# Indexer keys of the sample group: four page gathers and a DRAM round trip in place of 48 gathers and 32 register-addressed transfers

## The chip, the cores and the metric

The kernel runs on one core of one Trainium2 chip. The metric is the device time of one execution in microseconds, as the median of three runs. The kernel before takes 2734.93 us (2734.37 to 2735.12).

## What is computed

The reference is one inference step of a two-layer decoder trunk: layer 0 is sparse attention with an indexer, layer 1 a convolution module, each followed by a gated feed-forward block with a short convolution. A prompt of 256 tokens and a sample group of 8 sequences with 4 tokens each go through the same weights, 288 columns in all. Only the indexer of the sample group touches the change: each sequence has 2048 past positions in 16 pages of 128, and the pages lie anywhere in a pool of 160.

```python
ki_past = cache_ki[page_table].reshape(Bd, PAST_LEN, IDX_DIM)       # 8 x 2048 x 64
dots  = jnp.einsum('thd,sd->ths', qi, ki, ...)                      # 16 index heads
score = jnp.einsum('th,ths->ts', wi * IDX_W_SCALE, jax.nn.relu(dots))
_, idx = lax.top_k(jnp.where(causal, score, -jnp.inf), k_sel)       # 256 of 2052
```

The keys and values at `idx` are then gathered and attended to. Everything else is matrix products with weights that are read once.

## The kernel before

**Products with weights.** `K.pump` (L135) loads a weight slab of 128 x 1024 numbers (512 KB) with one DMA on SP's queue (L145) into one of five `raw` buffers, then splits it into a high part `wh` (ACT, L159) and a low part `wl` (DVE, L161), three buffers of each. `K.gemm_gen` (L187) runs three matmuls of 288 columns for each 128 x 128 block: `wh` with `xh` (L228), `wh` with `xl` (L229), `wl` with `xh` (L230). A slab of the first stage has two rows of four blocks, 24 matmuls. While PE works on slab i, loads are issued up to slab i + 4 and splits up to slab i + 2; a split for slab i + 3 needs the buffers that PE frees when it has finished slab i.

**Order of the other work.** All instructions are issued in the order of the program text. Side work is written as Python generators in lanes (`Lane`, L103). Each step of a product calls `tick` (L167), which adds the step's estimated time to every lane's credit (at most 3.0); a lane with positive credit runs its generator to the next `yield`, and the yielded number is taken off the credit. In one tick the lanes come in the order `ev`, `norms`, `bg`, `bg2`. So a `yield 6.0` means: go on after about 6 us worth of matmuls, by the program's own estimate. An engine then executes its instructions strictly in this order, and a wait in one holds what is behind it on that engine.

**The first stage** runs `g_idx[0]` (L732, slabs 0 and 1, 80 columns: index key and head weights), `g_idx[1]` and `g_idx[2]` (L1028, eight slabs each, index queries: slabs 2 to 9 and 10 to 17), then `g_k`, `g_q`. The lane `ev` turns the new index keys (`ropes`, L688) and then stores them: `post_ki` (L735) issues `out_kidx` on POOL's queue (L738). The lane `bg` holds `load_kx` (L670) and behind it `sample_index` (L802), whose 16 index products read the past index keys `kx` (L833).

**The past index keys.** `kiT` holds each page transposed, 64 rows of 128 numbers (512 bytes a row). Four tiles `kx[pr]` of 128 x 2048 hold two sequences each, 64 partitions per sequence, positions along the row. Twelve of the 16 pages of each sequence come by 48 gathers on POOL's queue (L665 to L668, through `gather`, L659): one gather fetches 128 rows of 512 bytes by a table of row numbers `idxI` (L647 to L652) and fills one 128 x 128 block. The last four pages of each sequence come by 32 transfers on SP's queue (L670 to L679): SP loads the page number from `tab` into a register (`value_load`, L676) and issues a DMA of 64 x 512 bytes from that address (L677). Two of these come with each step of the generator, between the weight loads on the same queue.

Of the kernel before, what the change touches and what calls it, by code (L numbers as in the profile page):

```python
# [7 lines left out]
F32 = mybir.dt.float32  # L8
F32R = mybir.dt.float32r
BF = mybir.dt.bfloat16  # L10
I32 = mybir.dt.int32
I16 = mybir.dt.int16
AF = mybir.ActivationFunctionType
OP = mybir.AluOpType
# [5 lines left out]
NS, TS = 8, 4  # L20
T = TP + NS * TS
NH, HD, NKV, GQ = 16, 128, 4, 4
NI, ID = 16, 64
PAST, PAGE = 2048, 128
NPG = PAST // PAGE
POOL = 160
# [14 lines left out]
CAP = 3.0  # L41
SDEL = 6
TOPK = 2.6
KG = 12
DGP = 6.0
NDG = 14
CQ = 287
BIS = (1.6, 0.2)
DOTS = 0.35
ROPE = 0.8  # L50
# [483 lines left out]
def trunk(ctx, tc, a, o, stages=9):  # L534
    k = K(ctx, tc, a, o)
    nc = k.nc
# [61 lines left out]
    ap = st.enter_context(tc.tile_pool(name="attn", bufs=1))  # L598
# [9 lines left out]
    bp = stB.enter_context(tc.tile_pool(name="idx", bufs=1))  # L608
# [7 lines left out]
    def split_tiles(j, n):  # L616
        for i in range(j, j + n):
            k.split_x(xh[:, i, :T], xl[:, i, :T], xs[:, i])
# [7 lines left out]
    load_x(12, 4)  # L626
    tab = bp.tile([128, 128], I32, name="tab")
    pt = a["page_table"]
    io = bp.tile([128, 3], F32, name="io")
    nc.gpsimd.dma_start(tab, bass.AP(tensor=pt.tensor, offset=pt.offset, ap=[[0, 128], [1, 128]]))  # L630
    nc.gpsimd.dma_start(io, a["iota"])
    coni = bp.tile([128, 2 * T], F32, name="coni")
    con = bp.tile([128, NCO], F32, name="con")

# [8 lines left out]
    split_tiles(0, 1)  # L643
    k.pump(-2)
    split_tiles(1, 3)

    tabI = bp.tile([128, 4, NPG], I32, name="tabI")  # L647
    idxI = bp.tile([128, 64], I32, name="idxI")
    tab3 = tab.rearrange("p (b g) -> p b g", g=NPG)
    for s in range(2):  # L650
        nc.vector.tensor_copy(tabI[s * 64:(s + 1) * 64], tab3[s * 64:(s + 1) * 64, s::2, :])
    nc.vector.tensor_scalar(idxI, tabI.rearrange("p a b -> p (a b)"), float(ID), io[:, 2:3], op0=OP.mult, op1=OP.add)  # L652
    split_tiles(4, 4)
    k.pump(-1)
    nc.sync.dma_start(coni, a["consts_i"])
# [3 lines left out]
    def gather(out, src, idx):  # L659
        nc.gpsimd.indirect_dma_start(out=out, out_offset=None, in_=src,  # L660
                                     in_offset=bass.IndirectOffsetOnAxis(ap=idx, axis=0))


    kx = [kvA.tile([128, 2, 1024], F32, name="kvt").rearrange("p a b -> p (a b)") for _ in range(4)]
    for g0 in range(0, KG, 2):  # L665
        for pr in range(4):
            for g in range(g0, g0 + 2):
                gather(kx[pr][:, g * 128:(g + 1) * 128], a["kiT"], idxI[:, pr * NPG + g:pr * NPG + g + 1])  # L668

    def load_kx():  # L670
        kp = a["kiT"].rearrange("(a d) c -> a d c", d=ID)
        for pr in range(4):
            for g in range(KG, NPG):
                for s_ in range(2):
                    c = (2 * pr + s_) * NPG + g
                    r = nc.sync.value_load(tab[0:1, c:c + 1], min_val=0, max_val=POOL - 1)  # L676
                    nc.sync.dma_start(kx[pr][64 * s_:64 * s_ + 64, g * 128:(g + 1) * 128],  # L677
                                      kp[bass.ds(r, 1)].rearrange("a d c -> d (a c)"))
                yield 2.9  # L679

    k.bg.append(load_kx())

# [119 lines left out]
    def sample_index():  # L802
# [63 lines left out]
        nc.vector.tensor_scalar(scr, S, 0.0, 0.0, op0=OP.is_ge, op1=OP.add, accum_out=cnt)  # L866
        yield BIS[0]
        p = total()
        yield BIS[1]
        nc.vector.tensor_scalar(v, p[:, :1], float(KSEL_S), -1.0, op0=OP.is_lt, op1=OP.mult)  # L870
        for bit in range(30, -1, -1):
# [4 lines left out]
            nc.vector.tensor_scalar(scr, S, cand.bitcast(F32), 0.0, op0=OP.is_ge, op1=OP.add, accum_out=cnt)  # L876
            yield BIS[0]
            p = total()
            yield BIS[1]
            fl = sp.tile([128, 1], I32, name="fl", bufs=2)  # L880
# [8 lines left out]
        nc.vector.tensor_scalar(eq, S, thr, 0.0, op0=OP.is_equal, op1=OP.add, accum_out=ce)  # L889
        yield BIS[0]  # L890
        p = total()
# [179 lines left out]
    for gi in range(2):  # L1071
# [6 lines left out]
        for tt in range(3):  # L1078
            n = 128 if tt < 2 else 32
            p = bank("tr", 3)  # L1080
# [182 lines left out]
    for t in range(n_t + 1):  # L1263
        if t == n_t - 8:
            k.pump(g_out[0].first)
        if t < n_t:
            if t % TS == 0:
                b = t // TS
# [256 lines left out]

    spread = tc.dram_tile([last * 128, CQ], F32, name="spread")
    zero = fp.tile([128, last, CW], F32, name="zero")
# [178 lines left out]
def _consts():  # L1706
    f = np.float32
    c = np.zeros((128, NCO), f)

    def put(n, v, p0=0):  # L1710
        o_, w_ = CO[n]
        c[p0:p0 + v.shape[0], o_:o_ + w_] = v

    p = np.arange(128)
    same = (p[:, None] % 32) == (p[None, :] % 32)
    put("bones", same.astype(f))
    put("lower", (same & (p[:, None] // 32 < p[None, :] // 32)).astype(f))
    hrow = (p % 64) // TS
    put("esel", (np.arange(NI)[:, None] == hrow[None, :]).astype(f), 64)
    tok = (2 * np.arange(4)[None, :, None] + (p // 64)[:, None, None]) * TS + (p % TS)[:, None, None]  # L1720
    put("wmask", ((tok == np.arange(32)[None, None, :]) * IDX_W).astype(f).reshape(128, 128))
    pos = np.concatenate([np.arange(TP), np.tile(PAST + np.arange(TS), NS)]).astype(f)

    def angles(rot):
        inv = np.power(f(500000.0), (-np.arange(0, rot, 2, dtype=f) / f(rot)).astype(f)).astype(f)
        ang = (pos[:, None] * inv[None, :]).astype(f)
        return np.cos(ang).T.astype(f), np.sin(ang).T.astype(f)

    cs, sn = angles(32)
    put("cq", np.tile(np.concatenate([cs, cs]), (4, 1)))  # L1730
    put("sq", np.tile(np.concatenate([-sn, sn]), (4, 1)))
    cs, sn = angles(16)
    ci = np.concatenate([np.tile(np.concatenate([cs, cs, np.ones((48, T), f)]), (2, 1)),
                         np.tile(np.concatenate([-sn, sn, np.zeros((48, T), f)]), (2, 1))], axis=1)
    put("tri", (p[None, :] > p[:, None]).astype(f))
    put("ncaus", np.where(np.arange(TS)[None, :] <= (np.arange(32) % TS)[:, None], 0.0, NEG).astype(f), 96)
    r = np.arange(32)
    put("blk", (r[:, None] // TS != r[None, :] // TS).astype(f), 96)
    put("oneb", ((p % 32)[:, None] // TS == np.arange(NS)[None]).astype(f))
    put("seg", np.tile(-float(PAGE) * np.arange(4, dtype=f), (128, 1)))  # L1740
    put("pow", np.tile(2.0 ** np.arange(8), (128, 1)).astype(f))
    put("tapm", (p[:, None] % 32 == np.arange(32)[None]).astype(f))
    put("tokr", np.where(r[:, None] == np.arange(144)[None] // GQ, NEG, 0.0).astype(f), 96)
    iota = np.stack([p, p % 32, p % 64], 1).astype(f)
    return c, np.ascontiguousarray(ci), iota, np.arange(512, dtype=f)


def _layout(inp):
    g = {n: np.asarray(v) for n, v in inp.items()}
    c = np.ascontiguousarray  # L1750
    a = {}
    a["xT"] = c(np.concatenate([g["x_prompt"].reshape(TP, D), g["x_sample"].reshape(NS * TS, D)]).T)
    a["kvc"] = np.concatenate([g["cache_k"][0].reshape(POOL * PAGE, NKV * HD),
                               g["cache_v"][0].reshape(POOL * PAGE, NKV * HD)], axis=1)
    a["kiT"] = c(g["cache_kidx"][0].transpose(0, 2, 1)).reshape(POOL * ID, PAGE)
    sc = np.zeros((D, NS, CW - 1 + TS), np.float32)
    sc[:, :, :CW - 1] = g["state_conv"][0].transpose(2, 0, 1)
    a["scT"] = c(sc.reshape(NT, 128, -1).transpose(1, 0, 2)).reshape(128, -1)
    a["stT"] = c(g["state_ffn"].transpose(0, 3, 1, 2)).reshape(2, FF, NS * 2)
    a["page_table"] = c(g["page_table"]).reshape(-1)  # L1760
    for n in ("w_attn_in", "w_attn_out", "w_pw1", "w_pw2"):
        a[n] = c(g[n][0])
    for n in ("w_ffn_gate", "w_ffn_up", "w_ffn_down"):
        a[n] = c(g[n])
    cols = {}
    fm = lambda v: v.reshape(-1, 128).T
    for n in ("b_pw1", "b_dw", "ln_conv_g", "ln_conv_b", "b_pw2"):
        cols[n] = fm(g[n][0])
    for n in ("ln_mix_g", "ln_mix_b", "ln_ffn_g", "ln_ffn_b"):
        for l in range(2):  # L1770
            cols[f"{n}{l}"] = fm(g[n][l])
    cols["w_dw"] = g["w_dw"][0].reshape(CW, NT, 128).transpose(2, 1, 0).reshape(128, NT * CW)

    wq = np.concatenate([np.zeros((1, D), np.float32), g["w_dw"][0]]).reshape(8, 4, NT, 4, 32)
    a["w_dq"] = c(wq.transpose(1, 4, 2, 3, 0).reshape(128, NT * 32))
    for l in range(2):
        cols[f"w_c{l}"] = g["w_ffn_conv"][l].reshape(3, NF, 128).transpose(2, 1, 0).reshape(128, NF * 3)
        cols[f"b_c{l}"] = fm(g["b_ffn_conv"][l])
    a["pvec"] = c(np.concatenate([cols[n] for n in PV], axis=1))
    a["consts"], a["consts_i"], a["iota"], a["iota512"] = _consts()  # L1780
    a["ident"] = np.eye(128, dtype=np.float32)
    return a

# [38 lines left out]
```

## Time and profile before

| | us |
|---|---|
| median of 3 runs | 2734.93 |
| the profiled execution, its own time | 2738.89 |
| span of the profiled execution, first to last instruction | 2737.1 |
| PE busy (matmul) | 2597.2 (95%) |
| DVE busy | 1570.6 (57%) |
| ACT busy | 1138.6 (42%) |
| POOL busy | 653.5 (24%) |

The page cuts the span into 40 slices of 68.4 us and gives for each the busy share of every engine in tenths, the clock that PE was granted, and how busy the 16 DMA engines were. PE is the engine to read first. A stretch of a timeline gives, for each instruction or run of equal ones, the start, the time taken, the engine, the line, the operation with its tiles, and in brackets how long the engine had been idle before and what ended that idle time; "issue" means that the profile shows nothing that it waited for. A table by windows gives the busy time of PE, PEld (weight load), DVE, ACT and POOL in a stretch with the number of instructions, then PE's granted clock, the share of the DMA engines' time in use and what they moved.

### The profile page before, as it was taken

The numbers are of one execution on the slowest core, as the hardware profiler recorded it, in microseconds if no ns is written. First come the engines' busy times: TensorE is split into PE (matmuls) and PEld (weight loads), VectorE is DVE, ScalarE is ACT, GpSimd is POOL, SyncE is SP. The second block draws the span as 40 slices with busy tenths as digits, with TensorE's granted clock in tenths as the row PEclk, the third lists the DMA queues.
The fourth block names the chain that finished last, engine by engine and source line by source line (L and its number), as shares of the span: only waits on it lengthen the run. The fifth ranks groups of instructions, "written<-read, shape, count | busy, mean of one in ns | idle before, by whom it ended". The sixth has DMA issues, their size and how long they took to land. (4 is left out here: it accounts for less than half of the span.)

```text
span 2737.1 us, 50293 instructions
## 1 busy us (share of the span) xinstructions
PE 2597.2 (95%) x19976; PEld 2488.5 (91%) x19976; DVE 1570.6 (57%) x2417; ACT 1138.6 (42%) x1747; POOL 653.5 (24%) x841
## 2 busy tenths in 40 slices
PE   3899798999999999999999999999999999999997
PEld 2869765899999999999998788899999999999997
DVE  2458744569666545555557455777755544555554
ACT  1344343456444334444346332555544333444433
POOL 6116524134222110111135132435111000011023
PEclk6899899999999999999999999999999999999998
DMA  5524556555555555555644666455555545555653
GB/s 166 146 78 139 185 197 244 173 168 171 183 166 171 161 163 165 168 165 165 164 161 129 163 163 166 158 170 159 171 170 163 162 158 166 168 164 163 159 176 107
DMA packets 409275, 446.94 MB, mean 163 GB/s; under 512 B 35840, under 2 KB 337584, under 8 KB 408912
## 3 DMA queue, kind: packets, MB, share of 16 engines
q1 hardware_dynamic: 396256, 397.88, 48.5%
q0 software_dynamic: 12784, 45.85, 5.4%
q8 instruction: 156, 2.56, 0.4%
q14 instruction: 79, 0.65, 0.1%
HBM read 434.54 MB, written 9.10 MB: 162 GB/s over the span
## 5 line engine op out<-in xcount | busy, mean ns | idle before, releaser
L161 DVE TENSOR_TENSOR wl<-raw,wh 128x1024 fp32r<-128x1024 f32 (+2 forms) x693 | 861.1, 1246 | 922.1 <-ACT wh L159 862.1
L159 ACT ACTIVATE wh<-raw 128x1024 fp32r<-128x1024 f32 (+1 forms) x726 | 760.7, 1051 | 1043.4 <-PE pt L229 735.2
L229 PE MATMUL pt<-xl,wh 128*128 128x288 f32 (+1 forms) x3520 | 1046.0, 297 | 8.8 <-DVE xl L476 8.7
L228 PE MATMUL pt<-xh,wh 128*128 128x288 f32 (+1 forms) x3520 | 1044.5, 297 | 0.8 <-ACT xh L1286 0.8
L230 PE MATMUL pt<-xh,wl 128*128 128x288 f32 (+1 forms) x3520 | 1042.0, 296 | 1.6 <-DVE wl L161 1.6
L229 PEld LDWEIGHTS pt<-xl,wh 128*128 128x128 f32 x3520 | 666.1, 189 | 11.5 <-DVE xl L476 11.0
L228 PEld LDWEIGHTS pt<-xh,wh 128*128 128x128 f32 x3520 | 665.5, 189 | 7.4 <-issue 6.2
L230 PEld LDWEIGHTS pt<-xh,wl 128*128 128x128 f32 x3520 | 668.4, 190 | 2.1 <-DVE wl L161 2.1
L230 PE MATMUL pt<-hh,wl 128*128 128x288 f32 (+1 forms) x1664 | 495.3, 298 | 3.6 <-DVE wl L161 3.6
L229 PE MATMUL pt<-hl,wh 128*128 128x288 f32 (+1 forms) x1664 | 495.3, 298 | 0.0
L228 PE MATMUL pt<-hh,wh 128*128 128x288 f32 (+1 forms) x1664 | 493.2, 296 | 1.2 <-ACT wh L159 1.2
L230 PEld LDWEIGHTS pt<-hh,wl 128*128 128x128 f32 x1664 | 312.8, 188 | 5.1 <-DVE wl L161 5.1
L228 PEld LDWEIGHTS pt<-hh,wh 128*128 128x128 f32 x1664 | 314.0, 189 | 2.3 <-ACT wh L159 2.1
L229 PEld LDWEIGHTS pt<-hl,wh 128*128 128x128 f32 x1664 | 313.4, 188 | 0.2
L1402 POOL COPY sto<-gpad 128x2 f32<-128x2 f32 x88 | 82.0, 932 | 964.5 <-ACT gpad L1395 964.4
L228 PE MATMUL pg<-xh,wh 128*128 128x288 f32 (+1 forms) x464 | 151.7, 327 | 26.0 <-issue 15.6
L230 PE MATMUL pg<-xh,wl 128*128 128x288 f32 (+1 forms) x464 | 143.4, 309 | 19.2 <-issue 16.7
L229 PE MATMUL pg<-xl,wh 128*128 128x288 f32 (+1 forms) x464 | 143.5, 309 | 16.4 <-issue 16.2
L228 PEld LDWEIGHTS pg<-xh,wh 128*128 128x128 f32 (+1 forms) x464 | 92.9, 200 | 35.1 <-issue 23.9
L161 POOL TENSOR_TENSOR wl<-raw,wh 128x1024 fp32r<-128x1024 f32 x33 | 80.4, 2438 | 163.6 <-DVE S L854 104.3
L1406 ACT ACTIVATE s<-y,pvec 128x304 f32<-128x304 f32 x88 | 48.4, 550 | 161.9 <-DVE y L1401 161.9
L230 PEld LDWEIGHTS pg<-xh,wl 128*128 128x128 f32 (+1 forms) x464 | 92.8, 200 | 21.8 <-issue 18.4
(378 smaller groups left out, 2397.3 us busy)
## 6 DMA issues: line engine op xcount, KB each, us to landing
raw<-w_ffn_gate SPq DMA_DIRECT2D x352, 256.0 KB
raw<-w_ffn_up SPq DMA_DIRECT2D x352, 256.0 KB
raw<-w_ffn_down SPq DMA_DIRECT2D x169, 512.0 KB
raw<-w_attn_in SPq DMA_DIRECT2D x64, 512.0 KB
raw<-w_pw SPq DMA_DIRECT2D x128, 256.0 KB
raw<-w_attn_out SPq DMA_DIRECT2D x32, 512.0 KB
raw<-w_pw SPq DMA_DIRECT2D x32, 512.0 KB
xt<-spread SPq DMA_DIRECT2D x60, 142.0 KB
```

The source lines that it names most:

```text
L159: nc.scalar.activation(wh[:, :n], r[:, :n], AF.Copy)
L161: eng.tensor_tensor(wl[:, :n], r[:, :n], wh[:, :n].bitcast(F32), op=OP.subtract)
L228: nc.tensor.matmul(out, wh[:, c:c + w], xh, start=st, stop=False)
L229: nc.tensor.matmul(out, wh[:, c:c + w], xl, start=False, stop=False)
L230: nc.tensor.matmul(out, wl[:, c:c + w], xh, start=False, stop=sp)
L1402: nc.gpsimd.tensor_copy(sto[:, j, 0:2], gp[:, 256:258])
L1406: nc.scalar.activation(s[:, :304], y[:, :304], AF.Silu, bias=k.par(bc, j))
```

## The change

The table of row numbers and both kinds of transfer go. `kiT` is seen as rows of 16 index dimensions, a quarter of a page (8192 bytes). `pgi` holds one page number per partition (128 = 8 sequences x 16 pages), `pgq` four row numbers per partition (4 x page + quarter). Four gathers fetch the four quarters of all 128 pages, one page per partition. The four tiles are written side by side to a DRAM tile `kid`, one row of 32 KB per page, and eight transfers read it back in the layout that the index products want: for sequence b, 64 partitions, 16 pieces of 512 bytes in each. Writes and reads go on ACT's queue. All of it is in the generator `load_kx`, at places set by `KXD`. The index products and all that follows are as they were.

```diff
-KG = 12
+KXD = (6.0, 12.0, 12.0, 1.5)
...
-    io = bp.tile([128, 3], F32, name="io")
+    pgi = bp.tile([128, 1], I32, name="pgi")
...
-    nc.gpsimd.dma_start(io, a["iota"])
+    nc.gpsimd.dma_start(pgi, bass.AP(tensor=pt.tensor, offset=pt.offset, ap=[[1, 128], [1, 1]]))
...
-    tabI = bp.tile([128, 4, NPG], I32, name="tabI")
-    idxI = bp.tile([128, 64], I32, name="idxI")
     tab3 = tab.rearrange("p (b g) -> p b g", g=NPG)
-    for s in range(2):
-        nc.vector.tensor_copy(tabI[s * 64:(s + 1) * 64], tab3[s * 64:(s + 1) * 64, s::2, :])
-    nc.vector.tensor_scalar(idxI, tabI.rearrange("p a b -> p (a b)"), float(ID), io[:, 2:3], op0=OP.mult, op1=OP.add)
...
+    kid = tc.dram_tile([NS * NPG, ID * PAGE], F32, name="kid")
     kx = [kvA.tile([128, 2, 1024], F32, name="kvt").rearrange("p a b -> p (a b)") for _ in range(4)]
-    for g0 in range(0, KG, 2):
-        for pr in range(4):
-            for g in range(g0, g0 + 2):
-                gather(kx[pr][:, g * 128:(g + 1) * 128], a["kiT"], idxI[:, pr * NPG + g:pr * NPG + g + 1])
+    pgq = bp.tile([128, 4], I32, name="pgq")
+    for i in range(4):
+        nc.vector.tensor_scalar(pgq[:, i:i + 1], pgi, 4.0, float(i), op0=OP.mult, op1=OP.add)
+    kq = a["kiT"].rearrange("(a d) c -> a (d c)", d=ID // 4)
 
     def load_kx():
-        kp = a["kiT"].rearrange("(a d) c -> a d c", d=ID)
-        for pr in range(4):
-            for g in range(KG, NPG):
-                for s_ in range(2):
-                    c = (2 * pr + s_) * NPG + g
-                    r = nc.sync.value_load(tab[0:1, c:c + 1], min_val=0, max_val=POOL - 1)
-                    nc.sync.dma_start(kx[pr][64 * s_:64 * s_ + 64, g * 128:(g + 1) * 128],
-                                      kp[bass.ds(r, 1)].rearrange("a d c -> d (a c)"))
-                yield 2.9
+        yield KXD[0]
+        for i in range(4):
+            gather(kx[i], kq, pgq[:, i:i + 1])
+        yield KXD[1]
+        for i in range(4):
+            nc.scalar.dma_start(kid[:, 2048 * i:2048 * i + 2048], kx[i])
+        yield KXD[2]
+        for b in range(NS):
+            nc.scalar.dma_start(kx[b // 2][64 * (b % 2):64 * (b % 2) + 64].rearrange("d (g c) -> d g c", c=PAGE),
+                                kid[b * NPG:(b + 1) * NPG].rearrange("g (d c) -> d g c", c=PAGE))
+            yield KXD[3]
```

## Rows read from the trace of the kernel before

**Rows 1.** The page: PE's busy tenths and granted clock in 40 slices.
```profile
PE   3899798999999999999999999999999999999997
PEclk6899899999999999999999999999999999999998
```
**Rows 2.** Windows 22.9 to 84.8 and 84.8 to 139 us (columns as described above).
```profile
22.90:84.80 61.90, 13.96 (x47) 11.28 (x46) 8.61 (x20) 3.71 (x4) 42.20 (x52) 0.53 0.33 96
84.80:139.00 54.20, 53.86 (x397) 52.60 (x397) 32.89 (x62) 19.95 (x25) 0.00 (x0) 1.00 0.57 168
```
**Rows 3.** Timeline of PE: slab 2 begins, matmuls before, in and after the slow stretch.
```profile
17.12 0.36 PE L228 MATMUL pg<-xh,wh 128*128 128x288 f32 x1
...
22.84 0.29 PE L230 MATMUL pg<-xh,wl 128*128 128x288 f32 x1
22.97 0.30 PE L228 MATMUL pg<-xh,wh 128*128 128x288 f32 x1
...
27.73 0.40 PE L229 MATMUL pg<-xl,wh 128*128 128x288 f32 x1 [1.80 <-issue]
30.53 0.40 PE L230 MATMUL pg<-xh,wl 128*128 128x288 f32 x1 [2.40 <-issue]
...
79.97 0.44 PE L228 MATMUL pg<-xh,wh 128*128 128x288 f32 x1
80.22 0.44 PE L229 MATMUL pg<-xl,wh 128*128 128x288 f32 x1
...
84.95 0.30 PE L228 MATMUL pg<-xh,wh 128*128 128x288 f32 x1
```
**Rows 4.** Timeline of SP's queue, the x loads, then page transfers in and after the slow stretch.
```profile
3.45 5.15 SPq L614 DMA_DIRECT2D x<-xT  x2
...
45.98 8.49 SPq L677 DMA_DIRECT2D kvt<-kiT  x2
...
83.00 1.73 SPq L677 DMA_DIRECT2D kvt<-kiT  x2
```
**Rows 5.** Timeline of POOL: the first and the last of 48 gathers.
```profile
11.02 1.08 POOL L660 DMA_INDIRECT kvt<-kiT,idxI  x1 [7.53 <-DVE idxI L652]
...
71.52 0.94 POOL L660 DMA_INDIRECT kvt<-kiT,idxI  x1 [0.30 <-issue]
```
**Rows 6.** The instructions on `kiT`: their durations (least, median, most), first and last start.
```profile
L677 SPq DMA_DIRECT2D kvt<-kiT x32: 3/479/1397, 13.1 to 112.3; - x32
```
**Rows 7.** Timelines of POOL and PE around a later burst of 14 gathers.
```profile
321.67 1.07 POOL L660 DMA_INDIRECT kvt<-kvc,idxS  x1 [8.10 <-DVE idxS L964]
...
338.43 0.94 POOL L660 DMA_INDIRECT kvt<-kvc,idxS  x1 [0.30 <-issue]
...
335.19 0.29 PE L230 MATMUL sc<-xh,wl 128*128 128x288 f32 x1 [0.31 <-issue]
...
341.61 0.58 PE L228 MATMUL sc<-xh,wh 128*128 128x288 f32 x1 [0.33 <-issue]
```
**Rows 8.** Timelines: DVE's store of the new index keys, and the first index product.
```profile
27.07 0.30 DVE L737 COPY ki<-kiw 64x288 f32<-64x288 f32 x1
...
139.01 1.10 PE L833 MATMUL pg<-kvt,qiblk 128*128 128x512 f32 x2 [0.19 <-issue]
```
**Rows 9.** Windows with gathers, 512-byte pieces, a DRAM write, and weight loads alone.
```profile
330.00:345.00 15.00, 11.08 (x63) 10.20 (x62) 3.57 (x3) 4.10 (x6) 7.36 (x9) 0.77 1.03 405
1486.00:1488.00 2.00, 2.00 (x18) 2.00 (x17) 2.00 (x4) 1.11 (x3) 2.00 (x3) 1.00 0.86 257
1759.50:1763.50 4.00, 4.00 (x19) 4.00 (x18) 2.76 (x6) 3.93 (x7) 1.90 (x3) 0.50 1.08 461
1737.00:1741.00 4.00, 4.00 (x55) 3.18 (x46) 0.58 (x2) 0.44 (x1) 0.00 (x0) 1.00 1.03 384
```
**Rows 10.** Timeline of SP's queue: a DRAM write, and reads that wait for it.
```profile
1504.66 0.34 SPq L1583 DMA_DIRECT2D spread<-apad  x1
...
1506.80 1.76 SPq L1593 DMA_DIRECT2D xt<-spread  x4
```

More of the change, by code (lines that the diff above doesn't have):

```diff
@@ L1743, in _consts @@
     put("tokr", np.where(r[:, None] == np.arange(144)[None] // GQ, NEG, 0.0).astype(f), 96)
-    iota = np.stack([p, p % 32, p % 64], 1).astype(f)
-    return c, np.ascontiguousarray(ci), iota, np.arange(512, dtype=f)
+    return c, np.ascontiguousarray(ci), np.arange(512, dtype=f)
 def _layout(inp):
@@ L1779, in _layout @@
     a["pvec"] = c(np.concatenate([cols[n] for n in PV], axis=1))
-    a["consts"], a["consts_i"], a["iota"], a["iota512"] = _consts()
+    a["consts"], a["consts_i"], a["iota512"] = _consts()
     a["ident"] = np.eye(128, dtype=np.float32)
```

## The prediction

> **What bounds the kernel now.** I read the page first: PE is at nine tenths or more in nearly every slice, at nearly full clock, so the time is PE's, and a change counts if it gives PE time back or takes it away [rows 1]. The exception is the first slice (0 to 68 us): 3, with the clock at 6. The windows show what lies there: from 22.9 to 84.8 us PE starts 47 matmuls, in the next 54.2 us it starts 397 [rows 2]. At the later pace (397 / 54.2 = 7.32 per us) 47 matmuls are 6.4 us of work, so 55.5 us of PE's time are lost in this stretch. That is the prize.
>
> What PE waits for I looked up in its timeline. Up to 22.97 us the matmuls follow each other at 0.13 us; from 27.73 on one comes every 2.8 us, and the idle time before each ends with "issue", that is, with nothing the profile shows; from 79.97 on matmuls come every 0.24 us, which is the lower clock, and at 84.95 full pace is back [rows 3]. So this is no wait for weights. SP shows the same thing: the two table transfers from 45.98 take 8.49 us, such a pair at 83.00 takes 1.73 [rows 4]. In the same stretch POOL goes through its 48 gathers without a break, the first at 11.02, the last at 71.52 us [rows 5]: the slow stretch begins about 12 us after the first gather and ends about 7 us after the last.
>
> Two things run there that the change takes away: the gathers and SP's register-addressed transfers. Which of them slows PE and SP? The transfers go on to 112 us [rows 6], and PE is at full pace from 85 on [rows 2]; and much later, where 14 gathers go out in a row from 321.67 to 338.43 and there are no register loads, the same idle times with "issue" come up in PE at 335.19, 13.5 us after the first gather, and the last that I find is at 341.61, 2.2 us after the last gather's end [rows 7]. So I take a run of more than about ten gathers as the cause. I don't know by what path it acts, and need not: either suspect goes.
>
> **What the change removes.** The 48 gathers become four; at the pitch of the 48, (71.52 - 11.02) / 47 = 1.29 us [rows 5], they are issued in 5 us, well below the 12 us after which both slow stretches began. I count the whole 55.5 us as given back, to a start of slab 6 at about 31 us: slab 2 begins at 17.12 [rows 3], a slab is 24 matmuls (3.3 us), four slabs make 30.2, and I round up to 31. SP loses 32 register loads and 32 small DMAs; nothing else is late there, since its weight loads are then ahead of PE by the five buffers. DVE loses three small operations and gains four; nothing at this scale. Work behind stays in the same program order, so what follows slab 20 moves forward as a block.
>
> **What it adds: a chain through ACT.** By the credits, `load_kx` runs its first step in slab 0 (0.3675 x 8 = 2.94 us of credit, 6.0 taken), gathers in the first step of slab 2, writes 16 steps of 0.735 later, in slab 6, and reads in slabs 10 to 13. In slab 2's tick the lane `ev` comes before `bg`, so `out_kidx` now stands ahead of the gathers on POOL. It waits for the new index keys, which DVE has at 27.4 us [rows 8]; that chain hangs on early weight slabs, so I put the gathers at 26 us instead of 11, with 25 to 28 as bounds. The memsets behind the gathers come earlier than before, which costs nothing.
>
> Price of the trips, each 4.19 MB, on all DMA engines. The gather: nothing shows rows of 8192 bytes, the nearest window has gathers of 4096-byte rows at 405 GB/s and a full share: 10.4 us. The write: a DRAM write ran at 461 GB/s in a full window: 9.1 us. The read back in 512-byte pieces: 257 GB/s at a share of 0.86, so 299 at full share: 14.0 us [rows 9]. Together 33.5 us, all extra but for the 4.19 MB that went before too. Weight loads alone run at 384 GB/s [rows 9], 1.37 us for each slab of 3.3 us, so 58% of the engines are free beside PE at full pace. Then the gathers alone need 10.4 / 0.58 = 18 us and land by 44; the first writes, which start as soon as the first tile is there, share with them, so I say 47 to 48 us for the last gather.
>
> [...]
>
> **Where the chain shows.** ACT executes in order. It comes to the four writes after the split of slab 8, which it can do once PE is through slab 5, at 31 us, and there it waits for each gather in turn, to 47 or 48. Behind it wait the splits of slabs 9 and on. PE has slabs 6, 7 and 8 in its buffers, 9.8 us, so it stops at about 41 and goes on after the next split (1.06 us) at about 49 to 50: **a stop of 9 us**. After it, the lower clock: after the slow stretch PE took 5 us (79.97 to 84.95) at 0.24 us a matmul [rows 3], a loss of 2.2 us; I add the same. The second wait, of the reads for all four writes, comes in slab 10; by the same fair sharing the writes land at about 53 (PE stands still, so weights leave the engines free), while ACT gets there, with slab 9 done, at 54. A dependent read followed a DRAM write by 2.14 us [rows 10], and that is in it. So nothing there; bounds 0 and 6 us. The reads, 14.0 / 0.58 = 24 us, land by about 82; the index products, at 139 now [rows 8], come up at 139 - 55.5 + 11.2 = 95. Hidden, with 13 us to spare.
>
> Not seen in the trace: ACT as an issuer of DMAs. Its 12 issues at SP's 0.34 to 0.44 us each [rows 10] would be 5 us spread over seven slabs, beside 20 us busy of 54 [rows 2]: hidden. The nearest row for an issue that is held back is SP's pair of x loads, 5.15 us with many transfers outstanding [rows 4]; with one more split behind it such a hold is still inside the cover of three slabs. Bounds 0 and 4 us.
>
> [...]
>
> **The sum**, against the profiled execution: 2738.9 - 55.5 + 9 + 2.2 = 2694.6 us. The median of the runs lies 4.0 below the profiled execution, so 2690.6: **2691 us**. The bounds: no stop at all (gathers land before 41) is 2679, and slabs 2 and 3 a little earlier with less traffic 2677. At the other end a stop of 20 (gathers and writes at a third of the engines each), 6 for the writes, 4 for held issues and twice 2.2 for the clock, 34 in all: 2710.
>
> **Rivals.** *The slow stretch follows the gathers' outstanding bytes, not their number.* For it: only two stretches were seen, and both also had data on the way all the time. Against: the second had eight times the bytes per gather and began after the same 12 to 13 us. Price: gathers outstanding from 26 to 48, slow from 38 to 55. This covers the stop (41 to 50), and PE loses 17 plus 2.2 instead of 11: 2699, up to 2715 with the held waits. Still faster.
>
> *The slow stretch isn't the gathers' or the transfers' doing but belongs to the start of the program.* For it: PE's idle times name no releaser. Against: the later burst. Then nothing comes back, and ACT's waits lie inside the stretch: 2735, within 0.2%.
>
> *Slower: the three trips are too slow and the index products wait.* These stand in PE's order, so a late read back stops everything behind. The chain starts at 26; the gain is gone if it ends at 139, when 12.6 MB have moved at less than 111 GB/s. For it: in the stretch from 22.9 to 84.8 the engines moved just 96 GB/s in all, at a share of 0.33 [rows 2], and there two kinds of table transfer were running, one of them paced by POOL. At 96 GB/s the chain takes 131 us and ends at 157: 18 us later than now, 2753. Against: the same engines moved 405 GB/s where gathers had large rows [rows 9].
>
> **Chances.** Forecast 0.74, the stretch following the bytes 0.13, the start 0.05, too slow 0.08. A measurement of this kernel can tell 0.2% (5.5 us) from no change. Faster 0.87, same 0.05, slower 0.08. The range takes the forecast's bounds and the first rival: 2677 to 2716.
>
> **What would show it.** In the profile after: matmuls at 0.13 us through 23 to 41 us; four gathers on POOL from about 26 us, after `out_kidx`; ACT idle from about 32 until about 48, ended by a DMA into `kx`, and PE stopped for about 9 us ended by DVE or ACT; a lower clock for about 5 us; the first index product at about 95 us, ended by something other than a DMA; the 14-gather stretch near 290 us still there with its idle times. Wrong, if PE's 2.8 us pitch is still there with four gathers, if PE waits at the index products, or if the wait for the writes is the longer one.

## The result and the profile after

The changed kernel took **2701.65 us** (median of four runs, 2697.19 to 2707.67) beside 2734.65 for the kernel before on the same chip: a ratio of 0.9883, 95% interval 0.9863 to 0.9904. The profiled execution took 2701.6 us with a span of 2699.8. The forecast was 2691, its range 2677 to 2716. Of all executions below one is left out, of the run with 24 tiny gathers more: it took 3962.59 us at a mean granted clock of 0.58, where the others of that run had 0.98.

The page: PE's busy tenths, the granted clock and the DMA share in 40 slices.

```profile
PE   6998798999999999999998999999999999999997
...
PEclk8999998999999999999998999999999999999999
DMA  9534764656555455555645666455555445555643
```

The first slice (0 to 67.5 us) has gone from 3 to 6 for PE and from 6 to 8 for the clock, and its DMA share is 9; [rows 1] is the same of before. PE's 6 is still no 9, so something remains there. Windows tell where (busy time and count of PE, PEld, DVE, ACT and POOL, then granted clock, DMA share, GB/s):

```profile
41.00:52.50 11.50, 0.81 (x7) 0.58 (x5) 0.10 (x1) 1.19 (x2) 1.40 (x4) 0.68 1.01 417
52.50:58.70 6.20, 5.79 (x23) 5.44 (x24) 3.49 (x3) 3.00 (x5) 4.33 (x5) 0.50 1.02 388
58.70:72.00 13.30, 13.15 (x99) 12.92 (x99) 10.76 (x24) 4.54 (x5) 0.00 (x0) 1.00 1.06 242
72.00:90.00 18.00, 15.71 (x105) 15.24 (x104) 5.44 (x5) 5.68 (x9) 0.00 (x0) 0.91 1.14 278
```

PE stands still in the first, runs at a granted clock of 0.50 in the second, is at full pace in the third, and in the fourth starts 105 matmuls in 18 us where full pace would be some 132 (7.32 per us). The 2.8 us pitch [rows 3] is not there any more. The timelines of POOL, ACT (ACTq: its queue of DMA issues) and PE name what is:

```profile
26.11 0.58 POOL L735 DMA_DIRECT2D out_kidx<-ki  x1 [22.63 <-DVE ki L733]
26.99 1.06 POOL L654 DMA_INDIRECT kvt<-kiT,pgq  x1 [0.30 <-issue]
...
32.30 0.94 POOL L654 DMA_INDIRECT kvt<-kiT,pgq  x1 [0.30 <-issue]
...
32.54 18.67 ACTq L671 DMA_DIRECT2D kid<-kvt  x4
51.31 2.95 ACT L159 ACTIVATE wh<-raw 128x1024 fp32r<-128x1024 f32 x3 [18.21 <-DMA kvt<-kiT,pgq]
...
65.42 4.87 ACTq L674 DMA_DIRECT2D kvt<-kid  x2
...
70.42 8.60 ACTq L674 DMA_DIRECT2D kvt<-kid  x2
79.14 2.95 ACT L159 ACTIVATE wh<-raw 128x1024 fp32r<-128x1024 f32 x3 [7.68 <-PE pg L230]
...
52.42 0.61 PE L228 MATMUL pg<-xh,wh 128*128 128x288 f32 x1 [10.69 <-ACT wh L159]
...
102.53 1.10 PE L830 MATMUL pg<-kvt,qiblk 128*128 128x512 f32 x2 [0.17 <-issue]
...
303.07 0.29 PE L230 MATMUL sc<-xh,wl 128*128 128x288 f32 x1 [1.59 <-issue]
```

Four gathers go out behind `out_kidx` in 6 us (before: 48 in 61 us, [rows 5]). ACT sits in the four writes from 32.54 to 51.21, since each waits for its gather, and PE, out of split weights, stands for 10.69 us until ACT splits again. Later two pairs of the reads hold ACT for most of 4.87 and 8.60 us, and the splits behind them come late: PE waits 1.57 us for ACT at 80.25 and 0.73 us for DVE at 81.51, and after it the granted clock is 0.71 from 80.2 to 86.1 us. The first index product starts at 102.53 us instead of 139.01 [rows 8], 36.5 us earlier, and waits for nothing: the keys are hidden. In the later burst of gathers PE still has its idle times with "issue" [rows 7].

### The profile page after: what moved, and what is told of

Read it like the earlier page. It is cut to its first block, busy times and chain, and to the rows that moved or that the text cites. A ratio compares the mean times of both kernels' runs of the same rounds, so it can differ in the third digit from the quotient of the medians.

```text
span 2699.8 us, 50043 instructions
## 1 busy us (share of the span) xinstructions
PE 2592.8 (96%) x19976; PEld 2485.7 (92%) x19976; DVE 1569.6 (58%) x2418; ACT 1137.9 (42%) x1747; POOL 613.9 (23%) x797
```

## Experiments

Times are medians. The kernel before ran beside every set of kernels: 2732.7, 2664.4, 2730.1, 2664.6 and 2731.4 us for the five sets, in this order. That the second and the fourth are 66 us lower is a finding of its own and is taken up below; each kernel is compared with the kernel before of its own set.

**Which of the two causes the slow stretch? All gathers, or none.** Set one (before: 2732.7).

```diff
-KG = 12
+KG = 16
```

> The kernel before with all 64 pieces fetched by gathers (64 in a row on POOL) and no register-addressed transfer on SP; same result. Theory (a run of more than about ten gathers slows PE): 16 more gathers at 1.29 us make the slow stretch 20 us longer, its end moves from 84.8 to about 105 us, and the time is about 2755. Rival (SP's register-addressed transfers slow PE): the 2.8 us pitch is gone, PE is at full pace from 23 us on, and the time is about 2735 - 55.5 = 2680. Rival (it belongs to the start of the program): end of the stretch and time as before, 2735.

Measured: 2745.87 us, ratio 1.0042 (1.0024 to 1.0061). A window in the slow stretch, and the timelines of POOL (first and last gather) and PE (the end of the stretch):

```profile
60.00:80.00 20.00, 3.20 (x8) 2.29 (x8) 0.00 (x0) 0.00 (x0) 15.12 (x17) 0.50 0.19 53
```

```profile
11.27 1.10 POOL L660 DMA_INDIRECT kvt<-kiT,idxI  x1 [7.79 <-DVE idxI L652]
...
93.17 0.95 POOL L660 DMA_INDIRECT kvt<-kiT,idxI  x1 [0.30 <-issue]
...
101.99 0.40 PE L229 MATMUL pg<-xl,wh 128*128 128x288 f32 x1 [2.40 <-issue]
102.19 0.44 PE L230 MATMUL pg<-xh,wl 128*128 128x288 f32 x1
```

Without any register-addressed transfer the pitch is still there, and with 16 gathers more it ends at 102, 22 us later than the 79.8 of before. The time rose by 13 us only, where 20 were expected, since in this run the stretch was milder at first: in 20 to 40 us PE started 61 matmuls (33 in before), in 40 to 60 us 16 (7). Why it was milder is not shown; the register-addressed transfers, which are missing here, may have made it worse.

```diff
-    for g0 in range(0, KG, 2):
...
-                gather(kx[pr][:, g * 128:(g + 1) * 128], a["kiT"], idxI[:, pr * NPG + g:pr * NPG + g + 1])
+    for pr in range(4):
+        nc.gpsimd.memset(kx[pr][:, :KG * 128], 0.0)
```

> The kernel before with its 32 register-addressed transfers as they were, but without the 48 gathers: three quarters of the index keys are not fetched, four memsets on POOL fill their place with zeros. Theory (the gathers slow PE): no 2.8 us pitch, PE at full pace through 23 to 85 us, time 2735 - 55.5 = 2680. Rival (the register-addressed transfers): the stretch is there as before, 2735. Rival (the start of the program): the stretch is there as before, 2735.

Measured: 2680.25 us, and PE starts 427 matmuls where it started 47 [rows 2]. The register-addressed transfers are all there. So **the gathers make the slow stretch, the register-addressed transfers don't**, nor does the start of the program.

```profile
22.90:84.80 61.90, 59.09 (x427) 58.11 (x426) 39.91 (x73) 22.29 (x27) 7.53 (x12) 0.97 0.63 190
```

**What the change would be worth without its trip through DRAM.** Same set.

```diff
-        yield KXD[1]
-        for i in range(4):
-            nc.scalar.dma_start(kid[:, 2048 * i:2048 * i + 2048], kx[i])
-        yield KXD[2]
-        for b in range(NS):
-            nc.scalar.dma_start(kx[b // 2][64 * (b % 2):64 * (b % 2) + 64].rearrange("d (g c) -> d g c", c=PAGE),
-                                kid[b * NPG:(b + 1) * NPG].rearrange("g (d c) -> d g c", c=PAGE))
-            yield KXD[3]
```

> The changed kernel with its four gathers alone: the writes to DRAM and the reads back are left out, so the index products use keys in the wrong order. Theory: what the change gives back is the whole slow stretch and what it adds all hangs on ACT's twelve transfers, so PE runs from 23 to 100 us without a stop: 2735 - 55.5 = 2679, 22 below the changed kernel. Of these, the stop and its lower clock make 14 us and the held reads 4 to 5 by the trace of the changed kernel, which would give 2683. Rival (the gathers of 4.19 MB crowd out weight loads by themselves): PE waits for weights between 27 and 45 us, and the time is over 2690.

Measured: 2679.81 us, 52.9 below the kernel before. The first window again, now with the four gathers (4.19 MB in all) in it: PE waits for none of them.

```profile
22.90:84.80 61.90, 59.80 (x443) 58.52 (x442) 40.22 (x78) 22.64 (x28) 11.62 (x16) 1.00 0.70 238
```

**Is it the number of gathers?** Same set.

```diff
+    sc8 = bp.tile([128, 24 * 8], F32, name="sc8")
+    k8 = a["kiT"].rearrange("a (e c) -> (a e) c", c=8)
...
         for i in range(4):
             gather(kx[i], kq, pgq[:, i:i + 1])
+        for i in range(24):
+            gather(sc8[:, 8 * i:8 * i + 8], k8, pgq[:, i % 4:i % 4 + 1])
```

> The changed kernel with 24 more gathers behind its four, each of 128 rows of 32 bytes (4 KB, 98 KB in all) into a tile that nobody reads; all else as it was. Theory (the number of gathers in a row): POOL issues 28 gathers from 27 to about 64 us, the 2.8 us pitch comes up at about 39 to 40 us and ends between 66 and 71; ACT's stop (41.5 to 52.4) lies inside it, so PE loses about 28 us instead of 14 there: 2702 + 14 = 2716, between 2711 and 2726. Rival (the outstanding bytes): 98 KB beside 4.19 MB are nothing, no such pitch, 2702 within 3.

Measured: 2701.34 us, and no 2.8 us pitch from 20 to 115 us; the longest wait of PE with "issue" there is 0.6 us. **My theory fell here**: 28 gathers made no slow stretch. The rival on bytes had it right (2702 within 3), but so would another reading: POOL waited twice (to 44.5 and to 50.2 us), and the 16 gathers after that went out from 51.47 to 73.58, one per 1.47 us, where before had one per 1.25. POOL's timeline, and the window of 60 to 80 us:

```profile
51.47 0.95 POOL L654 DMA_INDIRECT sc<-kiT,pgq  x1 [0.30 <-issue]
52.72 1.96 POOL L654 DMA_INDIRECT sc<-kiT,pgq  x1 [0.30 <-issue]
...
73.58 0.94 POOL L654 DMA_INDIRECT sc<-kiT,pgq  x1 [0.30 <-issue]
```

```profile
60.00:80.00 20.00, 18.15 (x125) 16.64 (x124) 11.42 (x24) 3.18 (x3) 12.83 (x13) 1.00 1.15 225
```

**The bytes, or the pace? Tiny gathers in the places of the 48.** Set three (before: 2730.1).

```diff
+    k8 = a["kiT"].rearrange("a (e c) -> (a e) c", c=8)
+    for pr in range(4):
+        (nc.gpsimd if pr < 2 else nc.vector).memset(kx[pr][:, :KG * 128], 0.0)
...
-                gather(kx[pr][:, g * 128:(g + 1) * 128], a["kiT"], idxI[:, pr * NPG + g:pr * NPG + g + 1])
+                gather(kx[pr][:, g * 128:g * 128 + 8], k8, idxI[:, pr * NPG + g:pr * NPG + g + 1])
```

> The kernel before with its 48 gathers in the same places, each fetching 32 bytes a row instead of 512 (4 KB instead of 64 KB a gather); the rest of the keys is zeros, written by two memsets each on POOL and DVE ahead of them. Of the 28 gathers of the run with tiny gathers no slow stretch came. Theory A (it needs the bytes of the gathers, 64 KB each): no 2.8 us pitch, about 2680 where before takes 2733. Theory B (it needs a run of gathers early in the program, or more than 28): the pitch comes up at about 28 us, as before; 2733 to 2738. Where before takes 2664 the run tells nothing of this.

Measured: 2728.57 us, ratio 0.9998 (0.9987 to 1.0010). With a sixteenth of the bytes the slow stretch is there again. PE's first wait with "issue" ends at 34.61 us (24.11 in before), as the gathers come in a row only from 22.45 on, and the last at 84.18 (79.78). Timelines of POOL and PE:

```profile
18.92 3.23 POOL L660 DMA_INDIRECT kvt<-kiT,idxI  x1 [1.80 <-DVE kvt L667]
22.45 0.95 POOL L660 DMA_INDIRECT kvt<-kiT,idxI  x1 [0.30 <-issue]
...
76.18 0.94 POOL L660 DMA_INDIRECT kvt<-kiT,idxI  x1 [0.30 <-issue]
...
58.19 0.40 PE L229 MATMUL pg<-xl,wh 128*128 128x288 f32 x1 [2.40 <-issue]
...
83.47 0.40 PE L229 MATMUL pg<-xl,wh 128*128 128x288 f32 x1 [2.39 <-issue]
84.18 0.40 PE L230 MATMUL pg<-xh,wl 128*128 128x288 f32 x1 [0.31 <-issue]
```

So not the bytes either. What is left is the pace, and the tails say how: the last idle time ends at 341.61 behind 14 gathers from 321.67 [rows 7], at 79.8 behind 48 from 11.02, at 101.99 behind 64 from 11.27. Divided by the count, (end - first gather) / gathers is 1.42, 1.43 and 1.42 us; with the tiny gathers, counted from the one at 22.45, it is (84.18 - 22.45) / 43 = 1.44. **It is as if each gather left something that takes 1.42 us to work off, and POOL issued one per 1.25 us.** By this reading what is behind piles up, and once it has piled up PE's and SP's instructions wait; a gather per 1.47 us piles up nothing. The next run tests it.

**Pace: the same gathers, half of them spaced.** Set five (before: 2731.4).

```diff
+    gap = bp.tile([128, 96], F32, name="gap")
...
                 gather(kx[pr][:, g * 128:(g + 1) * 128], a["kiT"], idxI[:, pr * NPG + g:pr * NPG + g + 1])
+                for _ in range(4 if g0 >= KG // 2 else 0):
+                    nc.gpsimd.memset(gap, 0.0)
```

> The kernel before with its first 24 gathers as they were (pitch 1.25 us) and four memsets of 128x96 behind each of the last 24 (pitch about 2.1 us, the last at about 91 us); same result. A backlog that grows by what a gather needs beyond its pitch fits the tails so far: (60.5 + 8) / 48 = 1.43 us a gather before, (82 + 10) / 64 = 1.44 with 64, (16.8 + 2.2) / 14 = 1.36 in the later burst; 28 gathers of which the last 18 went out at 1.47 us made none. Theory (backlog at some 1.42 us a gather): the slow stretch starts at about 24 us and ends 5 to 12 us after the last unspaced gather, at 46 to 53, while gathers still go out; PE is at full pace from there to the index products; where before takes 2730 this takes 2695 to 2710. Rival (the count in a row, whatever the pitch): the 2.8 us pitch lasts to about 98 us, over 2740. Rival (neither on this chip): where before takes 2664, PE is at full pace through 24 to 46 us with 24 gathers at 1.25 us behind each other, which shows that the stretch is missing there and with it what the change gives back; the keys come late then, 2675 to 2680.

Measured: 2702.53 us, ratio 0.9902 (0.9882 to 0.9922), in the middle of what the backlog gives. The timelines of POOL and PE, and a window behind the stretch:

```profile
42.08 0.95 POOL L660 DMA_INDIRECT kvt<-kiT,idxI  x1 [0.30 <-issue]
43.02 0.90 POOL L671 MEMSET gap<- 128x96 f32 x4
44.08 0.95 POOL L660 DMA_INDIRECT kvt<-kiT,idxI  x1 [0.15 <-issue]
...
91.97 0.95 POOL L660 DMA_INDIRECT kvt<-kiT,idxI  x1 [0.16 <-issue]
...
49.22 0.40 PE L230 MATMUL pg<-xh,wl 128*128 128x288 f32 x1 [1.70 <-issue]
...
52.85 0.40 PE L230 MATMUL pg<-xh,wl 128*128 128x288 f32 x1 [0.82 <-issue]
53.05 0.44 PE L228 MATMUL pg<-xh,wh 128*128 128x288 f32 x1
```

```profile
60.00:80.00 20.00, 20.00 (x152) 20.00 (x152) 10.65 (x20) 8.58 (x11) 17.05 (x46) 1.00 0.74 225
```

PE's slow matmuls end at 52.85 us, 11 us after the last gather at the old pace, while 19 gathers are still to come, one per 2.15 us; with these going on beside it PE is at full pace (152 matmuls in 60 to 80). By 52.85, 29 gathers had gone out from 10.79 on: 42.06 / 29 = 1.45 us each.

**All 48 spaced.** Set four (before: 2664.6).

```diff
+    gap = bp.tile([128, 96], F32, name="gap")
...
                 gather(kx[pr][:, g * 128:(g + 1) * 128], a["kiT"], idxI[:, pr * NPG + g:pr * NPG + g + 1])
+                for _ in range(2):
+                    nc.gpsimd.memset(gap, 0.0)
```

> The kernel before with its 48 gathers in the same order and size, but with two memsets of 128x96 into a small tile behind each gather on POOL, which stretch the pitch of the gathers from 1.25 to about 1.65 us (the last at about 90 us); same result. The slow stretch came with 48 gathers at a pitch of 1.25 us, of 64 KB and of 4 KB each, and with 64; it did not come with 28 of which the last 18 went out at 1.47 us. Its tail after the last gather grew with the count: 2 us behind 14, 7 to 8 behind 48, about 10 behind 64. Theory (something that every gather leaves behind is worked off more slowly than a gather per 1.25 us, and while it is behind, every engine's instructions wait): at 1.65 us it keeps up, no 2.8 us pitch, PE at full pace through 23 to 80 us, 2680 to 2690 where before takes 2730 (the keys may come some us late for the first index products). Rival (the count in a row, whatever the pitch): the slow stretch starts at about 24 us and lasts to about 97, and the time is over 2740. Where before takes 2664 the run tells nothing of this.

Measured: 2678.90 us, ratio 1.0049 (1.0033 to 1.0066). This set had the lower time for the kernel before, so it tells nothing of the pace, as the expectation has it. What it shows is the price of spacing: the last keys are asked for at 93.46 us, and PE stands for 11.43 us at an index product. That product is the first, and its own keys were asked for some 10 us earlier. What it waited for is its other input, `qiblk`: POOL's memset of this tile stands behind all the gathers, and DVE's copies into it wait 10.39 us for POOL. (Timeline of all engines.)

```profile
95.83 0.54 POOL L782 MEMSET qiblk<- 128x512 f32 x1
...
96.41 1.70 DVE L813 COPY qiblk<-qi 64x128 f32<-64x128 f32 x4 [10.39 <-POOL S L783]
...
98.32 2.05 PE L836 MATMUL pg<-kvt,qiblk 128*128 128x512 f32 x2 [11.43 <-issue]
```

**What the trip costs, and whose queue it is on.** Set two (before: 2664.4).

```diff
-            nc.scalar.dma_start(kid[:, 2048 * i:2048 * i + 2048], kx[i])
+            nc.gpsimd.dma_start(kid[:, 2048 * i:2048 * i + 2048], kx[i])
...
-            nc.scalar.dma_start(kx[b // 2][64 * (b % 2):64 * (b % 2) + 64].rearrange("d (g c) -> d g c", c=PAGE),
+            nc.gpsimd.dma_start(kx[b // 2][64 * (b % 2):64 * (b % 2) + 64].rearrange("d (g c) -> d g c", c=PAGE),
```

> The changed kernel with the four writes and the eight reads issued by POOL instead of ACT; same result. Theory (what is left of the price is ACT standing still, 14 us at the writes and 4 to 5 at the reads): POOL waits for the gathers instead, with nothing behind it that PE needs before its rotations of the index queries; PE does not stop at 41 us, time about 2702 - 18.5 = 2683. Rival (the transfers fill the DMA engines, whoever issues them): PE waits for weights between 41 and 87 us, at most 5 us are won, 2697 or more. Rival (POOL's held issues take longer than ACT's and the index products wait for the keys): the first index product is ended by a DMA, and the time is 2690 to 2710.

```diff
-            nc.scalar.dma_start(kid[:, 2048 * i:2048 * i + 2048], kx[i])
+            nc.gpsimd.dma_start(kid[:, 2048 * i:2048 * i + 2048], kx[i])
```

> The changed kernel with only the four writes issued by POOL; the eight reads stay on ACT; same result. Theory: the stop of 41.5 to 52.4 us with its lower clock goes from the place of the writes, but ACT now comes to the reads in slab 10 at about 42 us, before the writes have landed (52 to 58), and stands still there: of 10.9 us of stop some 5 to 11 come back in slabs 10 to 13, so the time is 2692 to 2702, 9 or more above the kernel with all twelve on POOL. Rival (the cover of three slabs takes it): 2687 or less.

Measured: 2663.56 us with all twelve on POOL, 2685.10 with the writes alone; the kernel before took 2664.36 beside them (ratios 0.9991, 0.9981 to 1.0002, and 1.0077, 1.0062 to 1.0091). The absolute numbers were expected for the higher level of the kernel before, but the distance of 21.5 us between the two has the sign and about the size of the theory's (9 to 19): with only the writes moved, the stop has moved to the reads. In its trace ACT has done its last split at 46 us. The writes, which POOL issues from 48.07 us on, land from 54.1 to 61.5, the first read goes out at 61.66, and PE stands for 9.79 us:

```profile
61.66 1.37 ACTq L674 DMA_DIRECT2D kvt<-kid  x2
63.15 1.06 ACT L159 ACTIVATE wh<-raw 128x1024 fp32r<-128x1024 f32 x1 [16.88 <-issue]
...
64.26 0.61 PE L228 MATMUL pg<-xh,wh 128*128 128x288 f32 x1 [9.79 <-ACT wh L159]
```

**The changed kernel, the version on POOL and the kernel before on one chip.** Set three again (before: 2730.1).

> The changed kernel once more, beside the kernel before and the version with all twelve transfers on POOL on one chip. Its ACT stop (14 us with the clock) and held reads (4 to 5) do not hang on the slow stretch: 18 us above the version on POOL. Where before takes 2733 it is 33 us faster than before, where before takes 2664 it is 17 to 19 us slower.

> All twelve transfers on POOL, as before. Where before takes 2733: 2680 to 2685, as fast as the run with the gathers alone. Where before takes 2664: 2664, as in the call before.

Measured: 2695.51 us for the change (ratio 0.9865, 0.9845 to 0.9884) and **2680.65** for the version on POOL (0.9816, 0.9799 to 0.9832), 14.9 us apart where 18 were expected. The run with the trip left out had 0.9808 (0.9790 to 0.9826) in its own set: **on POOL's queue the trip costs nothing that these runs can tell.** The DMA engines are as full as with ACT, and PE doesn't notice (POOL's timeline, then two windows):

```profile
44.71 2.43 POOL L783 CAST selB<-con 32x256 bf16<-32x256 f32 x4 [10.53 <-DMA kvt<-kiT,pgq]
...
49.71 2.24 POOL L671 DMA_DIRECT2D kid<-kvt  x4
65.74 6.59 POOL L674 DMA_DIRECT2D kvt<-kid  x8 [13.79 <-DMA kid<-kvt]
```

```profile
40.00:60.00 20.00, 19.06 (x144) 18.82 (x143) 14.12 (x27) 7.58 (x11) 7.11 (x12) 1.00 1.00 381
60.00:80.00 20.00, 20.00 (x151) 19.64 (x149) 11.44 (x23) 7.78 (x10) 6.59 (x8) 1.00 1.04 295
```

POOL waits 10.53 us for the gathers and 13.79 for the writes, with nothing behind it that PE is waiting for.

**Why does the kernel before have two times?** Set three held the kernel before once more for its profile.

> The kernel before itself once more, for its profile on the chip of this call: the calls so far ran it at 2733 us on one chip and at 2664 on another. Theory (the slow stretch is what differs): where the time is near 2733 the trace has the 2.8 us pitch from about 23 to 85 us; where it is near 2664 PE is at full pace in 23 to 85 us and slab 20 starts at about 78 instead of 132 us. Rival (another part of the program is faster on that chip): the pitch is there at 2664 too.

Measured, in one execution: 2728.39 us, with the slow stretch (in 40 to 60 us PE starts 8 matmuls; the last idle time ends at 78.47, (78.47 - 10.36) / 48 = 1.42 us a gather again). The chip was the one on which the second set had 2664.4: **one and the same chip shows both.** There is no profile of the kernel before at 2664. But the version on POOL was profiled at either level, and there the difference can be seen: at 2680 PE has idle times with "issue" in its waits from 310 to 430 us, where gathers for the attention go out; at 2664 it has none, though there too the gathers go out 1.24 to 1.25 us apart where they come in a row. (Waits of PE: what waited, for what, us in total, times, longest. First at 2680, then at 2664.)

```profile
PE tr L1164 <- issue: 4.0, 3, 3.2
PE m L1228 <- issue: 2.2, 3, 1.0
PE q L1136 <- issue: 1.9, 3, 1.2
```

```profile
PE tr L1164 <- DMA kvx<-kvc,idxS: 3.2, 1, 3.2
```

Its span was 2676.1 and 2663.4 us, and 10.5 of these 12.7 us come up between 320 and 430 us. The other profiles agree: from 265 to 450 us, where the later gathers go out, PE has no wait with "issue" in the three profiles of the second and fourth set, and 2.9 to 12.3 us of them in each of the others. So in two of five sets gathers in a row did not slow the other engines.

For the kernel before this explains the two times: 2730 less the 53 of the slow stretch and the 13 (spans) to 17 (medians) of the later gathers is 2660 to 2664. Its granted clock bears this out: the mean over an execution was 0.985 to 0.990 at 2664 and 0.973 to 0.980 at 2730. A stretch of 61.9 us at 0.53 [rows 2] takes 0.47 x 61.9 / 2737 = 0.011 off the mean, about that distance, and the run without gathers had 0.985 to 0.988. It is still an inference for that kernel, seen in profiles of the others. What switches the condition stays open.

## Why the prediction was right, and where it was off

**The cause.** That the gathers make the slow stretch and that four of them do not is shown (no gathers: 2680; all gathers: stretch longer). That it is "a run of more than about ten" is wrong as a rule: 28 made none, and in the run with half of them spaced PE was at full pace with the last 19 going out. What counts, in the sets where the effect is present, is a pace above one per 1.42 us, and the ten gathers before the stretch would be what the pile needs to show. The forecast did not hang on this, as four gathers are few by either rule.

**What is given back, 55.5 us.** Measured: 52.9 in the run without the trip, and in the traces slab 20 starts at 78.51 there instead of 132.01 (53.5 us). The step that overdid it is the start of slab 6: 32.02, not 31, because slabs 2 to 5 took 14.6 us and not 14; another 1.3 us went in slabs 6 to 20, which took 46.5 us there and 45.2 in before.

**The stop, 9 us.** 10.69 us in the trace. The mechanism is as told, behind the very slab named (slabs 6 to 8 done at 41.5). What was mis-sized is the last gather: ACT was free at 51.2, not at 47 or 48. One us of this is the start of the gathers, 26.99 and not 26; through the rest gathers, first writes and weights shared the engines at 417 GB/s and a share of 1.01 (41 to 52.5 us). That ACT's writes share them with the gathers and the weights was my estimate; in the trace, from 30 to 57 us, the gathers' queue has 37.5% of the 16 engines' time, ACT's 36.8% and SP's 25.9%.

**The lower clock, 2.2 us.** The 5 us of before that this was taken from (79.97 to 84.95) had a granted clock of 0.51. After the stop slab 9 took 6.4 us instead of 3.2 at a granted clock of 0.50, a wait of 0.41 us for DVE included: 3.2 us.

**The second wait, none.** Right: ACT came to the first read at 59.36 and issued it in 0.66 us.

**Held issues, 0 of 0 to 4.** This is the term that was taken at the wrong end, and it came out just above its upper bound. The issues of reads 5 to 8 held ACT for up to 6.3 us, and slabs 14 to 17 took 17.1 us instead of 12.8: 4.3 us, of which 2.3 are PE's waits at 80.25 and 81.51 and the rest the lower clock after them. I had let one held issue hide behind three slabs of cover; there were four in a row.

The terms as measured in the trace: -53.5 + 10.7 + 3.2 + 4.3 = -35.3, beside 36.5 us by which slab 20 starts earlier (95.54 for 132.01) and 37.3 between the spans; one or two us are not accounted for, about what two runs of the same kernel differ by. The forecast had -44.3, 7.0 more than the spans give. The rest of the 10.65 us between 2691 and 2701.65 is the 4.0 that I took off for the median of before, less rounding; the profiled execution of after was at its own median.

**The bounds.** Two of the sums don't come out as written: a price of 34 us gives 2738.9 - 55.5 + 34.4 - 4.0 = 2714, not 2710, and the first rival with held waits of 6 and 4 us gives 2709, not 2715. The range hardly changes, and the measured time lies inside either.

**Luck.** That the comparison fell into a time when the effect of the gathers was present was luck. The prediction took the slow stretch as a property of the kernel; in two of five sets it was not there, and by the estimate below the change would then have been slower than the kernel before.

**The rivals.** Outstanding bytes: out, a sixteenth of the bytes made the same stretch. The start of the program: out, by the run without gathers. Index products that wait for their keys: not in the change. The wait of 11.43 us in the run with all gathers spaced looks like it, but was for the query tile behind POOL's gathers.

**Whose queue the trip is on.** The DMA share is full whoever issues (1.01 to 1.14 from 41 to 90 us with ACT, 1.00 and 1.04 from 40 to 80 us with POOL). Yet the same twelve transfers cost 14.9 us on ACT's queue (2695.51 - 2680.65) and nothing measurable on POOL's. In the trace of the change the waits for other transfers took 10.7 us and the lower clock behind them 3.2, and the issues themselves were not small: 2.1 to 6.3 us for each of the last four reads on ACT's queue, some 0.8 on POOL's, which cost the other 4.3 us.

## What to carry to other kernels

Where matmuls come every 2 to 3 us with "issue" as the only reason and SP's instructions stretch alike (to 0.70 us here), look at POOL: in three of five sets gathers in a row at 1.25 us did it. Four large gathers in place of 48 took it away, and at a pitch of 1.47 or 2.15 us it did not come or did not go on. A transfer that must wait for another belongs on the queue of an engine that nobody waits for (2680.65 us with the trip on POOL's queue, 2695.51 on ACT's); moving half of the chain only moved the stop (9.79 us of PE at the reads, where it had been 10.69 at the writes). And time the kernel before in several sets: here its own level moved by 66 us, more than the change is worth, and at the lower level the version on POOL was no faster than before (0.9991). The change itself was not run at that level; from its distance of 14.9 us to the version on POOL I estimate some 2678 us there, slower than before.

## What the runs showed of the hardware

- A gather of 128 rows took POOL 0.94 us and a pitch of 1.25; where the effect is present, 1.42 to 1.45 us a gather fit the end of the slow stretch behind 14, 29, 48 and 64 gathers, whether they brought 64 KB, (in the later burst) 512 KB or 4 KB each.
- In the stretch POOL's gathers took their usual 0.94 us, but nearly every instruction of SP took about 0.70, whatever it did: a register check (median 0.71 from 28 to 78 us, 0.018 from 85 us on) as well as the issue of a page transfer (median 0.70 from 28 to 78 us). Least, median and most of all the checks, in ns, stand below. PE's matmuls came mostly at 2.1, 2.8 or 3.5 us, three, four or five times 0.70. That each instruction, and not each byte or matmul, waited for a turn is my reading of these numbers; what is worked off at that pace, no run shows.

```profile
L676 SPq SEQ_ASSERT  x32: 3/18/709, 12.8 to 112.1; - x32
```

- The same reads from DRAM went out as packets of 504 bytes in the mean on ACT's queue (4.19 MB in 8320 packets, 57 to 90 us) and of 3617 on POOL's (3.49 MB in 965 packets, 72 to 95 us), and no faster for it: with the weight loads beside them 242 to 278 GB/s at a full share (1.06 and 1.14, 58.7 to 90 us) on ACT, 248 (1.04, 70 to 95 us) on POOL.
- Not tried: 28 gathers at the full pace, with no other transfers beside them.
